# The up projection's norm row turned after its sixth weight piece

## The chip, the cores and the metric

The kernel runs on one core of a Trainium2 chip. A core has TensorE (PE, the matrix products), VectorE (DVE), ScalarE (ACT), GpSimd (POOL) and SyncE (SP, which here issues most transfers). The metric is the device time of one execution in microseconds, the median of several runs; the kernel before takes 1119.6 us.

## The reference

One layer of a hybrid encoder block on 256 tokens of 2048 features, in float32. The part around the change is the gated channel mixer, which starts with an RMS norm of the residual stream `h`:

```
def rmsnorm(x, g):
    y = xf * lax.rsqrt(jnp.mean(xf * xf, axis=-1, keepdims=True) + EPS)
    return (y * g.astype(F32)).astype(x.dtype)
def conv_glu(hn, w_up, conv_w, conv_b, w_down):
    up = hn @ w_up
    gate, val = jnp.split(up, 2, axis=-1)
    gate = dwconv_centred(gate, conv_w, conv_b)
    return (jax.nn.gelu(gate, approximate=True) * val) @ w_down
...
h = h + rmsnorm(mix @ w_out, mix_norm_post)
h = h + rmsnorm(conv_glu(rmsnorm(h, ffn_norm_pre), ...), ffn_norm_post)
```

`w_up` has 2 x 5632 columns. The gate half goes through a three-tap convolution over positions and a Gelu, and is multiplied by the value half. A mixer stands ahead of this part, the down projection and a gated per-layer embedding follow.

## The kernel before

**Precision.** Each float32 weight is split into a high part (rounded for the faster products, a cast on ScalarE, line 153) and a low part (the rest, a subtraction on VectorE, line 154). Two products, high by both parts of the activation (128x512) and low by the high part (128x256), stand for one float32 product.

**Pieces.** The up projection runs feature-major: features on partitions, the 256 tokens along the free axis. Its weights come in 176 pieces of 1024 columns of buffer. Four pieces (16 slices of 128 input features) make one block of 256 output features; `blocks` runs over slabs `s` of 512 features, first the two gate blocks `(s, 0, i)`, then the two value blocks `(s, 1, i)`. So pieces 0 to 3 are gate block 0 of slab 0 (tiles `ug_*`, results in `ga`), 4 to 7 gate block 1, and 8 to 15 the value blocks (`uv_*`, `va`). One transfer of 1 MB brings two pieces (`ug00r`, `ug01r`, `uv00r`, `uv01r`, two transfers each). There are three buffers for raw weights and five each for high and low parts (tags `raw`, `whi`, `wlo`), so a piece's high part takes over the buffer of the piece five before it. `next_part` splits a piece, five pieces ahead of its products; `feature_pairs` (line 355) issues the 16 products of a piece.

**The norm.** The products use `h` without the norm's factor per token; that factor is put on afterwards. `row_rstd` (line 398) squares and sums `h` per token on ScalarE (line 404) and takes the power -1/2 on POOL (line 381), with tokens on partitions. The gate needs the factor along the free axis. `along_tokens` (line 408) spreads each half over 128 columns (line 414, tile `rfbw`), turns it by a product with the identity (`mm`, line 90, tile `rfbp`), and copies it out (line 416, tile `rfb`). In the kernel before this is called ahead of the piece loop.

**A gate block's end.** `gate_out` adds the two partial results (lines 370 and 371) and multiplies by `rfb` (line 954). In the next block's first two passes of the loop come `gate_conv` (six ScalarE instructions, lines 961 to 963, and two VectorE additions, 964 and 965) and `gelu` (line 969). `value_out` multiplies the value by the gate. The value's factor is put on later, in the down projection.

**What sets the order.** Within `with in_order():` every instruction on ScalarE, VectorE and SyncE is tied to the one written before it on its engine. TensorE isn't in that list (`ORDERED`): its order is chosen by the scheduler when the kernel is built, under the data dependences and under `tc.issue_after(x)`, which ties what is issued inside it behind instruction `x`. `last["pe"]` is the product that was issued last. `jobs_at[n]` holds side work of pass `n`, block sums of later weights among it (`dnb`: fetch by SP, four additions at line 253, a store by POOL).

**Transfers ahead.** After the first split of the up projection SP's queue holds, in this order: `ug00r` twice, `ug01r` twice, two stores of `h` (`h_kept`), one of the embedding's half (`pl_kept`), `dnb`, `uv00r` twice, `dnb`, `uv01r` twice.

Of the kernel before, what the change touches and what calls it, by code (L numbers as in the profile page):

```python
# [11 lines left out]
F32 = mybir.dt.float32  # L12
F32R = mybir.dt.float32r
AF = mybir.ActivationFunctionType
ALU = mybir.AluOpType
ORDERED = (mybir.EngineType.Activation, mybir.EngineType.DVE, mybir.EngineType.SP)

P = 128
L = 256
# [34 lines left out]
def build(nc, a, out):  # L54
# [6 lines left out]
    with tile.TileContext(nc) as tc, \  # L61
# [9 lines left out]
        def ins(r):  # L71
            return getattr(r, "ins", r)
# [4 lines left out]
        def mid(name, dtype=F32):  # L77
            return gp.tile([P, 1024], dtype, tag="mid", bufs=3, name=name)
# [4 lines left out]
        def main(name):  # L83
            return [pm.tile([P, 512], F32, tag="main", name=f"{name}_{i}") for i in range(2)]

        def misc(name):
            return pc.tile([P, 512], F32, tag="misc", name=name)

        def mm(o, lhsT, rhs, start, stop):
            last["pe"] = ins(nc.tensor.matmul(o, lhsT, rhs, start=start, stop=stop, skip_group_check=True))  # L90
# [5 lines left out]
        ident = cp.tile([P, P], F32, name="ident")  # L96
# [9 lines left out]
        acc, acc2 = [main(f"dtu{t}") for t in range(2)], main("dtu2")  # L106
# [8 lines left out]
        last, sums_ = {}, {}  # L115
# [26 lines left out]
        def split(name, src, nel, cuts=()):  # L142

            if name in ready:
                return ready.pop(name)
            if name in spare:
                hi, lo = spare.pop(name)
            else:
                hi = wp.tile([P, 1056], F32R, tag="whi", bufs=5, name=f"{name}h")
                lo = wp.tile([P, 1056], F32R, tag="wlo", bufs=5, name=f"{name}l")  # L150
            for c0, c1 in zip((0, *cuts), (*cuts, nel)):
                s = slice(c0, c1)
                last["act"] = ins(nc.scalar.copy(hi[:, s], src[:, s]))  # L153
                last["dve"] = ins(nc.vector.tensor_sub(lo[:, s], src[:, s], hi[:, s].bitcast(F32)))
            return hi, lo

        def raw(name, src=None):
            r = wp.tile([P, 2048], F32, tag="raw", bufs=3, name=name)
            if src is not None:
                last["dma"] = load(r, src, True)  # L160
            return r
# [36 lines left out]
        @contextmanager  # L198
        def in_order():


            block = nc.cur_bb.bb.instructions
            seen = {i.name for i in block}
            yield
            for i in block:
                if i.name in seen or i.engine not in ORDERED:
                    continue
                if i.engine in chain:
                    tc.add_manual_dep(i, chain[i.engine].name,
                                      mybir.DependencyInfo(mybir.DependencyClass.NoSync, mybir.DependencyReason.DATA),  # L210
                                      reason="in_order")
                chain[i.engine] = i
# [142 lines left out]
        def feature_pairs(n, part, get, acc):  # L355

            wh, wl = part
            for kk in range(4):  # L360
                k = 4 * n + kk
                for f in range(2):
                    s = slice(kk * 256 + f * P, kk * 256 + (f + 1) * P)
                    mm(acc[f], wh[:, s], get.both(k), k == 0, False)
                    mm(acc[f][:, L:], wl[:, s], get(k)[0], False, k == NK - 1)

        def total(o, acc):

            for f in range(2):
                nc.scalar.copy(o[:, f * L:(f + 1) * L], acc[f][:, L:])  # L370
                nc.vector.tensor_add(o[:, f * L:(f + 1) * L], o[:, f * L:(f + 1) * L], acc[f][:, :L])
# [26 lines left out]
        def row_rstd(name, src):  # L398

            r = []  # L400
            for t in range(2):
                q = tiny(f"{name}q{t}", 1)
                junk = page(f"{name}j{t}")
                nc.scalar.activation(junk, src[t], AF.Square, accum_out=q)
                r.append(rms(f"{name}{t}", [q], 1.0 / D))
            return r

        def along_tokens(name, r):

            rb = sp.tile([P, L], F32, tag="rb", bufs=1, name=name)  # L410
            ps = misc(f"{name}p")
            for t in range(2):
                w = mid(f"{name}w{t}")
                nc.vector.tensor_copy(w[:, :P], r[t][:, 0:1].to_broadcast([P, P]))
                mm(ps[:, t * P:(t + 1) * P], w[:, :P], ident, True, True)
            nc.vector.tensor_copy(rb, ps[:, :L])
            return rb
# [283 lines left out]
        def job(f, *args):  # L701
            return lambda: f(*args)
# [75 lines left out]
        def gload(name, src):  # L778
            g = cp.tile([P, D], F32, tag="gain", name=name)
            load(g, src.partition_broadcast(P))  # L780
            return g
# [86 lines left out]
        for t in range(2):  # L868
            load(h[t], x[t * P:(t + 1) * P, :])
        hf = sublayer("wo", w_out, list(range(8, 16)) + list(range(8)), cat, gload("gmix", a["mix_norm_post"][0]), h,  # L870
                      V_FN, Pairs, ((5,), (2, 4)), Sums("cs", cat))
# [1 line left out]

        pl = [ple(0)]
        rf = row_rstd("rf", h)
        rfb = along_tokens("rfb", rf)
        h_kept = []
        for t in range(2):
            h_kept.append(dp.tile([P, D], F32, tag=f"h{t}", bufs=1, name=f"h_kept{t}"))
# [11 lines left out]
        for i, w_ in enumerate(which[2:] + which[:2]):  # L891
            fetch, add, store = block_sums(*w_, i >= len(which) - 2)
            n = 49 * i // 10 + 2
# [41 lines left out]
        blocks = [(s, v, i) for s in range(DFF // 512) for v in range(2) for i in range(2)]  # L935
        parts, slab = [], {}

        def next_part():

            n = len(parts)  # L940
            if n < NPIECES:
                s, v, i = blocks[n // 4]
                name = f"u{'gv'[v]}{s}{i}"
                if n % 2 == 0:
                    slab["raw"] = raw(f"{name}r{n // 2 % 2}", w_up[v, s, i, n // 2 % 2])
                parts.append(split(f"{name}{n // 2 % 2}_{n % 2}", slab["raw"][:, n % 2 * 1024:(n % 2 + 1) * 1024], 1024))

        def gate_out(s, i, acc):
            if i == 0:
                slab[s] = mid(f"gr{s}"), mid(f"fc{s}"), mid(f"ft{s}")  # L950
            o = slab[s][0][:, i * 512:(i + 1) * 512]
            total(o, acc)
            v = o.rearrange("p (f t) -> p f t", f=2)
            nc.vector.tensor_tensor(v, v, rfb.unsqueeze(1).to_broadcast([P, 2, L]), op=ALU.mult)

        def gate_conv(s, i):

# [13 lines left out]
        def value_out(s, i, acc):  # L971
# [4 lines left out]
            total(hd, acc)  # L976
            nc.vector.tensor_mul(hd, hd, slab[s][1][:, i * 512:(i + 1) * 512])

        with in_order():
            for _ in range(5):  # L980
                next_part()
            for n in range(NPIECES):
                s, v, i = blocks[n // 4]
                if n % 4 == 0:
                    acc = main(f"{'gv'[v]}a{s}{i}")
                feature_pairs(n % 4, parts[n], hf, acc)
                if n % 4 == 3:
                    (value_out if v else gate_out)(s, i, acc)
                next_part()
                if n >= 4 and n % 4 < 2 and blocks[n // 4 - 1][1] == 0:  # L990
                    (gelu if n % 4 else gate_conv)(blocks[n // 4 - 1][0], blocks[n // 4 - 1][2])
                for job in jobs_at[n]:
                    job()
# [98 lines left out]
        for half in range(2):  # L1092

            alt = [] if half else main(f"gts{half}")
            acc = [main(f"gt{half}{t}") for t in range(2)]
# [9 lines left out]
            for t in range(2):  # L1105
                for n, (o, c0) in enumerate(columns(acc[t])):
# [4 lines left out]
                    v = th[:, :c1 - c0]  # L1111
# [91 lines left out]
```

## Time and profile before

| what | us |
|---|---|
| median of 3 runs | 1119.6 (1119.28 to 1119.72) |
| the profiled execution | 1119.3 |
| its span in the trace | 1117.4 |
| TensorE busy | 1106.2 |
| VectorE busy | 946.9 |
| ScalarE busy | 718.0 |
| mean granted clock of TensorE | 0.998 |

The chain of waits, which goes back from the last instruction to what released each step, has 95% of its length on TensorE. Its pieces of gate and value blocks of the up projection take 43.4% of the span. One block of the steady part lies on it with 22.33 us per 128 products, which is two blocks of 64.

A row of the timeline gives the start in us, the duration in us, engine, line, operation, the tile written and the tiles read, and the shape and count; in brackets how long the engine had been idle and who released it. A TensorE duration includes the pipeline's fill, so that rows overlap: the pace is read from start to start. A row of a stage window gives the stretch, its length, the busy time (and instructions) of PE, its weight loads, DVE, ACT and POOL, the granted clock of TensorE, the DMA engines' share and GB/s. A row of the waits gives who waited for whom, total us, times and longest.

### The profile page before, as it was taken

To read this page: it belongs to the slowest core of one execution; us is meant where nothing else is said; L and a number is where in the kernel's file an instruction comes from. 1 tells how busy PE (TensorE), PEld (TensorE's weight loads), DVE (VectorE), ACT (ScalarE), POOL (GpSimd) and SP (SyncE) were. 2 spreads that over 40 slices of the span, in tenths; PEclk is the share of its full clock that TensorE was granted. 3 is DMA by queue.
4 is the path that set the end of the run, shared out by engine and by line. 5 is a ranking of instruction groups with operands and counts; after the bars stand their busy time and mean duration, and the time that the engine had idled before them with its cause. 6 is when DMAs were issued, how large, how long until landed. Compare 5 with 4: busy or idle time off the path is not lost.

```text
span 1117.4 us, 15979 instructions
## 1 busy us (share of the span) xinstructions
PE 1106.2 (99%) x5954; PEld 952.3 (85%) x5954; DVE 946.9 (85%) x1311; ACT 718.0 (64%) x1042; POOL 65.2 (6%) x134
## 2 busy tenths in 40 slices
PE   9999999999999999999999999999999999999997
PEld 9999988888888888888888888888888888877876
DVE  6468897799878898888878888889899999989795
ACT  7848663555775564665655646547689778867573
POOL 0200000100100000000000000000000000001001
PEclk9999999999999999999999999999999999999999
DMA  9752447454699999999899898999999799996663
GB/s 365 311 205 97 167 157 280 151 189 167 234 362 396 363 361 355 368 345 367 331 361 368 349 365 335 365 375 362 348 381 378 255 347 410 415 371 228 228 233 108
DMA packets 53503, 339.43 MB, mean 304 GB/s; under 512 B 5936, under 2 KB 6832, under 8 KB 19248
## 3 DMA queue, kind: packets, MB, share of 16 engines
q1 hardware_dynamic: 43488, 285.86, 66.2%
q0 software_dynamic: 9504, 51.91, 12.5%
q8 instruction: 47, 0.77, 0.3%
q10 hardware_dynamic: 432, 0.62, 0.2%
q14 instruction: 32, 0.26, 0.1%
HBM read 292.76 MB, written 45.61 MB: 303 GB/s over the span
## 4 chain that ended last, share of the span: by engine, by line
PE 95%; DVE 2%; ACT 2%; issue 1%; DMA 0%; POOL 0%; SPq 0%; POOLq 0%; ACTq 0%
PE va L90 22%; PE ga L90 21%; PE dna L90 12%; PE woa L90 7%; PE xbc L90 6%; PE gt L90 5%; PE z L90 4%; PE dtu L90 4%; PE dns L90 4%; PE dn0s L90 2%; PE dn1s L90 2%; PE ple L90 1%; PE pw L90 1%; PE yd L90 1%; DMA dtur<-w_dtu 0%
## 5 line engine op out<-in xcount | busy, mean ns | idle before, releaser
L90 PE MATMUL ga<-wox,ug_0h 128*128 128x512 f32 x352 | 125.5, 395 | 0.0
L90 PE MATMUL ga<-wox,ug_1h 128*128 128x512 f32 x352 | 125.1, 394 | 0.0
L90 PE MATMUL va<-wox,uv_0h 128*128 128x512 f32 x352 | 124.8, 393 | 0.0
L90 PE MATMUL va<-wox,uv_1h 128*128 128x512 f32 x352 | 124.7, 393 | 0.0
L90 PE MATMUL ga<-wox,ug_1l 128*128 128x256 f32 x352 | 99.2, 282 | 0.0
L90 PE MATMUL ga<-wox,ug_0l 128*128 128x256 f32 x352 | 99.1, 282 | 0.0
L90 PE MATMUL va<-wox,uv_0l 128*128 128x256 f32 x352 | 99.1, 281 | 0.0
L90 PE MATMUL va<-wox,uv_1l 128*128 128x256 f32 x352 | 98.9, 281 | 0.0
L253 DVE TENSOR_TENSOR dnb<-dnb 128x512 f32<-128x512 f32 x124 | 85.5, 690 | 3.2
L90 PEld LDWEIGHTS va<-wox,uv_0h 128*128 128x128 f32 x352 | 66.1, 188 | 15.0
L90 PEld LDWEIGHTS ga<-wox,ug_0h 128*128 128x128 f32 x352 | 66.1, 188 | 14.9
L90 PEld LDWEIGHTS ga<-wox,ug_1h 128*128 128x128 f32 x352 | 66.1, 188 | 14.9
L90 PEld LDWEIGHTS va<-wox,uv_1h 128*128 128x128 f32 x352 | 66.1, 188 | 14.9
L90 PEld LDWEIGHTS ga<-wox,ug_0l 128*128 128x128 f32 x352 | 66.2, 188 | 0.1
L90 PEld LDWEIGHTS va<-wox,uv_1l 128*128 128x128 f32 x352 | 66.2, 188 | 0.1
L90 PEld LDWEIGHTS ga<-wox,ug_1l 128*128 128x128 f32 x352 | 66.2, 188 | 0.0
L90 PEld LDWEIGHTS va<-wox,uv_0l 128*128 128x128 f32 x352 | 66.2, 188 | 0.0
L905 ACT CAST hs<-hid 128x512 fp32r<-128x512 f32 x44 | 27.3, 621 | 23.4 <-PE dna L90 23.1
L906 DVE TENSOR_TENSOR hs<-hid,hs 128x512 fp32r<-128x512 f32 x44 | 30.1, 685 | 8.3 <-ACT hs L905 8.3
L244 POOL DMA_DIRECT2D dns<-dnb x29 | 15.7, 540 | 318.4 <-DVE dnb L253 284.4
L90 PE MATMUL dna<-dn_0h,hs 128*128 128x512 f32 x104 | 33.1, 394 | 0.3 <-ACT dn_0h L153 0.3
L90 PE MATMUL dna<-dn_1h,hs 128*128 128x512 f32 x104 | 33.3, 393 | 0.0
(2164 smaller groups left out, 3168.4 us busy)
## 6 DMA issues: line engine op xcount, KB each, us to landing
dnb<-w_down SPq DMA_DIRECT2D x31, 1024.0 KB, 8.8
dns<-dnb POOLq DMA_DIRECT2D x29, 1024.0 KB, 5.3
hd<-hsum POOLq DMA_DIRECT2D x22, 512.0 KB, 8.2
zr<-w_z SPq DMA_DIRECT2D x8, 1024.0 KB, 5.0
dtur<-w_dtu SPq DMA_DIRECT2D x14, 528.0 KB, 8.4
wo0r<-w_out_ SPq DMA_DIRECT2D x7, 1024.0 KB, 4.9
dn1r<-w_down SPq DMA_DIRECT2D x7, 1024.0 KB, 6.8
wo1r<-w_out_ SPq DMA_DIRECT2D x6, 1024.0 KB, 4.9
```

Of the source, the lines that this page charges most:

```text
L90: last["pe"] = ins(nc.tensor.matmul(o, lhsT, rhs, start=start, stop=stop, skip_group_check=True))
L244: nc.gpsimd.dma_start(t, pg[0])
L253: nc.vector.tensor_add(v[:, i], v[:, i], v[:, j])
L905: nc.scalar.copy(t[:, :512], hid_part(k))
L906: nc.vector.tensor_sub(t[:, 512:], hid_part(k), t[:, :512].bitcast(F32))
```

## The change

The turned row is cut into three steps, `spread`, `turn` and `take`, which `norms_row` returns; nothing of it is issued ahead of the loop any more. `spread` (two copies on VectorE) is issued in pass 4, after that pass's split; `turn` (two products) in pass 5, behind the products of piece 5; `take` (the copy out) in pass 5 after its split. The products of piece 6 are tied behind the turning products. The norm of gate block 0 leaves `gate_out` and follows `take` in pass 5; its taps move from pass 4 to pass 6, its Gelu from pass 5 to pass 7. All other blocks keep their places; the norm is then read from `slab["rfb"]`. The spread row now takes the one buffer of tag `junk` in place of two tiles of `mid`.

```
-        rfb = along_tokens("rfb", rf)
+        def norms_row():
+            rb = sp.tile([P, L], F32, tag="rb", bufs=1, name="rfb")
+            ps = misc("rfbp")
+            w = sp.tile([P, 512], F32, tag="junk", bufs=1, name="rfbw")
+            def spread():
+                for t in range(2):
+                    nc.vector.tensor_copy(w[:, t * P:(t + 1) * P], rf[t][:, 0:1].to_broadcast([P, P]))
+            def turn():
+                with tc.issue_after(last["pe"]):
+                    for t in range(2):
+                        mm(ps[:, t * P:(t + 1) * P], w[:, t * P:(t + 1) * P], ident, True, True)
+            def take():
+                nc.vector.tensor_copy(rb, ps[:, :L])
+                slab["rfb"] = rb
+            return spread, turn, take
...
             total(o, acc)
-            v = o.rearrange("p (f t) -> p f t", f=2)
-            nc.vector.tensor_tensor(v, v, rfb.unsqueeze(1).to_broadcast([P, 2, L]), op=ALU.mult)
+            if s or i:
+                gate_norm(s, i)
+        def gate_norm(s, i):
+            v = slab[s][0][:, i * 512:(i + 1) * 512].rearrange("p (f t) -> p f t", f=2)
+            nc.vector.tensor_tensor(v, v, slab["rfb"].unsqueeze(1).to_broadcast([P, 2, L]), op=ALU.mult)
...
+        row = norms_row()
         with in_order():
...
-                feature_pairs(n % 4, parts[n], hf, acc)
+                with tc.issue_after(last["pe"]) if n == 6 else nullcontext():
+                    feature_pairs(n % 4, parts[n], hf, acc)
                 if n % 4 == 3:
                     (value_out if v else gate_out)(s, i, acc)
+                if n == 5:
+                    row[1]()
                 next_part()
-                if n >= 4 and n % 4 < 2 and blocks[n // 4 - 1][1] == 0:
+                if n == 4:
+                    row[0]()
+                elif n == 5:
+                    row[2]()
+                    gate_norm(0, 0)
+                elif n in (6, 7):
+                    (gelu if n == 7 else gate_conv)(0, 0)
+                elif n >= 8 and n % 4 < 2 and blocks[n // 4 - 1][1] == 0:
                     (gelu if n % 4 else gate_conv)(blocks[n // 4 - 1][0], blocks[n // 4 - 1][2])
```

## The prediction

> **What bounds the kernel now.** I read the engine totals first, then the chain of waits from 286 us on, then the waits of TensorE, then stage windows, and last each engine's timeline from 300 to 326 us.
>
> ```profile
> span 1117.4 us, 15979 instructions
> PE 1106.2 (99%) x5954; PEld 952.3 (85%) x5954; DVE 946.9 (85%) x1311; ACT 718.0 (64%) x1042; POOL 65.2 (6%) x134
> ```
> ```profile
> PE rfbp L90 <- DVE rfbw L414: 0.5, 1, 0.5
> ```
> ```profile
> 308.60:314.00 5.40, 5.40 (x33) 4.66 (x32) 3.14 (x6) 1.88 (x5) 0.74 (x2) 1.00 0.99 402
> 314.00:319.50 5.50, 5.50 (x33) 4.82 (x32) 2.60 (x3) 4.54 (x8) 0.00 (x0) 1.00 1.02 429
> 319.50:342.00 22.50, 22.50 (x131) 19.79 (x130) 21.78 (x28) 16.95 (x26) 1.33 (x2) 1.00 0.90 351
> 342.00:788.00 446.00, 446.00 (x2558) 391.49 (x2557) 377.81 (x514) 263.74 (x392) 23.39 (x44) 1.00 0.93 360
> ```
> TensorE (PE) is the bound. Its only wait near the change is 0.5 us for the spread row; from 308.6 to 788 us it never stops (first number after the length is PE's busy time). So no later hole can swallow a delay: what PE loses here moves the end. The DMA share, the last number but one, is 0.99 to 1.02 up to 319.5: the transfers are saturated.
>
> ```profile
> 307.13 0.40 PE L90 MATMUL ga<-wox,ug_0h 128*128 128x512 f32 x1
> 308.07 0.46 PE L90 MATMUL rfbp<-ident,rfbw 128*128 128x128 f32 x2 [0.54 <-DVE rfbw L414]
> 308.28 0.36 PE L90 MATMUL ga<-wox,ug_0l 128*128 128x256 f32 x1
> ...
> 310.23 0.49 PE L90 MATMUL rfbp<-ident,rfbw 128*128 128x128 f32 x2
> 310.47 0.48 PE L90 MATMUL ga<-wox,ug_0h 128*128 128x512 f32 x1
> ...
> 313.68 0.39 PE L90 MATMUL ga<-wox,ug_0h 128*128 128x512 f32 x1
> 313.91 0.28 PE L90 MATMUL ga<-wox,ug_0l 128*128 128x256 f32 x1
> 314.03 0.40 PE L90 MATMUL ga<-wox,ug_0h 128*128 128x512 f32 x1
> ```
> Durations overlap in the pipeline, so I price by start to start: a 512-wide product 0.23 us (313.68 to 313.91), a 256-wide one 0.12, a turning product 0.21 to 0.24. The row at 313.68 is the first of piece 6; a piece, eight of each kind, takes 2.8 us.
>
> **What is removed.** Between 307.36 (0.23 after the row at 307.13) and 313.68 PE spent 0.92 us up to 308.28 and 0.24 from 310.23 on the row. Both go from this place: piece 5 ends at 313.68 - 1.16 = 312.52. The 0.21 + 0.24 = 0.45 of products come back later; 0.71 is the most that the edit can win.
>
> **What is moved, and what it waits for.** PE is not in the hand-written order, so the compiled order of the changed kernel decides. Shortened, with the engine in front:
>
> ```
> PE   ... piece 5: ga_1<-wox,ug_1l
> PE   va_0<-wox,uv_0h [waits ACT]   va_1<-wox,uv_0h
> PE   va_0<-wox,uv_0l [waits DVE]   va_1<-wox,uv_0l   va_0 uv_0h   va_0 uv_0l   va_1 uv_0h
> PE   rfbp<-ident,rfbw [waits DVE]  rfbp<-ident,rfbw
> PE   piece 6, piece 7, the other 9 products of piece 8
> DVE  ug_1l, gr, gr, uv_0l (piece 8), uv_1l (piece 9), rfbw, rfbw, uv_0l (piece 10), rfb, gr norm
> ACT  gr, gr, uv_0h, uv_1h (8, 9), uv_0h (10), uv_1h (11), six taps
> ```
> Piece 6 is tied behind the turned row. Seven products of piece 8, not tied, were put ahead of the row; and on VectorE the two spreads stand behind the split of piece 9. So PE, which has pieces 6 and 7 ready to run, first waits for piece 8's weights and then for piece 9's split. When are those there?
>
> ```profile
> 305.24 0.43 SPq L120 DMA_DIRECT2D dnb<-w_down  x1
> 305.77 1.93 SPq L120 DMA_DIRECT2D uv00r<-w_up  x2
> ```
> ```profile
> DMA to landing us min/median/max: 9.0/9.8/10.6
> ```
> ```profile
> 314.89 1.05 ACT L153 CAST uv_0h<-uv00r 128x1024 fp32r<-128x1024 f32 x1 [4.41 <-DMA uv00r<-w_up]
> 316.80 0.60 ACT L961 ACTIVATE fc<-gr,vt 128x256 f32<-128x256 f32 x1
> ...
> 319.68 1.03 ACT L153 CAST uv_0h<-uv00r 128x1024 fp32r<-128x1024 f32 x1
> ```
> ```profile
> 307.69 0.23 DVE L414 COPY rfbw<-rf0r 128x128 f32<-128x128 f32 x1 [1.65 <-POOL rf0r L381]
> ...
> 315.98 1.22 DVE L154 TENSOR_TENSOR uv_0l<-uv00r,uv_0h 128x1024 fp32r<-128x1024 f32 x1 [2.28 <-ACT uv_0h L153]
> 317.12 1.22 DVE L154 TENSOR_TENSOR uv_1l<-uv00r,uv_1h 128x1024 fp32r<-128x1024 f32 x1
> ...
> 321.88 2.86 DVE L253 TENSOR_TENSOR dnb<-dnb 128x512 f32<-128x512 f32 x4
> ```
> The transfer uv00r is issued at 305.77 behind pl_kept and dnb and lands 9.0 us later; ScalarE stood idle 4.41 us for it. The edit changes no place and no wait in SP's queue, and the work of ScalarE and VectorE that frees its buffer and makes the value stored ahead of it lies before the first edited instruction. I keep the landing.
>
> Step by step: uv_0h is there at 314.89 + 1.05 = 315.94, PE starts at 316.0 (312.52 to 316.0: 3.5 us idle). Two 0.23 products, to 316.46. uv_0l is done at 315.98 + 1.22 = 317.20, so PE goes on at 317.25 (0.8 idle) with 0.12 + 0.12 + 0.23 + 0.12 + 0.23 = 0.82, to 318.07. The split of piece 9 starts at 317.12; the next instruction follows 1.14 later, as 317.12 follows 315.98: the first spread runs 318.26 to 318.49. Before, the turning product came 0.15 after the spread's end (307.69 + 0.23 = 307.92, to 308.07): now 318.64 (0.6 idle). Two of them, 0.45: piece 6 starts at 319.09 instead of 313.68, 5.41 later, but with 4 x 0.23 + 3 x 0.12 = 1.28 of piece 8 done. **Net 5.41 - 1.28 = +4.13 us.** The same by idle time: 3.5 + 0.8 + 0.6 = 4.9, less the 0.71 won, is 4.2. Bounds: the two uv00r transfers took 9.0 and 10.6 us, so a first one as slow as the second would add 1.6 us, and one 0.8 faster would take 0.8 off (every step behind the landing moves with it). The one issue that the edit brings forward, uv01r (its buffer no longer waits for a split behind the turned row), stands behind uv00r in the queue, so I take the 9.0.
>
> **What is late next, and what is free.** The six taps (316.80 to 319.68, 2.9 us), the norm and the Gelu move back by two pieces on ScalarE and VectorE. They hide behind the splits' lead of five pieces. The tightest is piece 11, whose high part needs the buffer of piece 6: free at 319.09 + 2.8 = 321.9, cast to 322.9 (1.05). Its low part stands behind the row's copy, the norm and the block sums (2.86), which have all run by then, and is done near 325. PE wants it after piece 7, the rest of 8, 9 and 10: 319.09 + 5.6 + 1.5 + 5.6 = 331.8, 7 us later. Piece 12's cast waits for the taps and two copies, until about 328, and is wanted at 334.6. So I price them at nothing; without the lead, the 2.9 us of taps would be paid. The stores on POOL's queue follow block sums that come about 1 us later or sooner, with nobody waiting for them in this stage.
>
> **The clock.** PE would work only 1.7 us of the 6.6 from 312.52 to 319.09. What does this trace do with so little work?
>
> ```profile
> 1.39 3.40 PE L109 MATMUL dtu<-ident 128*128 128x128 f32 x16 [1.39 <-POOL ident masks.py:199]
> 4.65 0.59 PE L90 MATMUL dtu<-dtu0h,hnh 128*128 128x352 f32 x2
> ...
> 293.60 0.60 PE L391 MATMUL woxt<-ident,h 128*128 128x128 f32 x4
> 293.95 0.48 PE L90 MATMUL ga<-wox,ug_0h 128*128 128x512 f32 x1
> ```
> ```profile
> 1021.55:1024.96 3.41, 2.62 (x16) 1.97 (x15) 3.41 (x6) 2.17 (x4) 0.00 (x0) 1.00 0.41 173
> 1106.88:1110.30 3.42, 2.66 (x18) 1.83 (x16) 1.51 (x4) 1.48 (x5) 0.82 (x2) 1.00 0.04 14
> 1110.30:1113.71 3.41, 1.13 (x2) 0.30 (x2) 2.08 (x3) 1.00 (x3) 0.55 (x1) 1.00 0.34 121
> 1113.71:1117.40 3.69, 0.00 (x0) 0.00 (x0) 0.00 (x0) 0.00 (x0) 0.00 (x0) 0.50 0.55 174
> ```
> The first transposes took 3.26 / 16 = 204 ns each, those at 293.60 0.35 / 4 = 88: a cold start at under half speed for some 3.3 us. At the end the granted clock fell to 0.50 after 3.41 us with 1.13 of work (a third), though PE had rested only 1.2 us; with 2.62 of 3.41 it held. In the new hole any stretch of 3.4 us that begins between 311.4 and 314.5 holds at most 1.1 us of work: if the clock is decided stretch by stretch, 3.1 of 3.4 ways in which they can lie drop it. So I expect a half-clock spell of some 3.3 us. It costs half of the work in it: at most 1.7, nothing where it falls on PE's waits. It begins between 314.8 and 317.9, and up to 319.1 most of it is waits: I take 0.9, about half, bounds 0 and 2.0 (1.7, and 0.3 for the products ahead of the row, which then hold it up).
>
> The Trainium skill, "TensorE: Matmul & The Clock Gate", Part 1, says that the clock drops to half after at least one idle window of about 3.4 us on a free-running grid. Read as a window with no work at all, it would hardly ever fit in the 3.5 us wait, and the sum would stay +4.1 (rival 1); the tail here dropped after a window a third busy, so I side with the row.
>
> **Sum.** +4.13 + 0.9 = +5.0. On the profiled execution's 1119.3 us (span 1117.4): 1124.3; the median of the runs shown lies 0.3 higher, so 1124.6.
>
> **Rivals.**
> 1. The stall comes, the clock holds: +4.1, 1123.7. For it: the third of work that dropped the clock is one case, at the end of the program. Against it: the stall has even less. Chance 0.25.
> 2. Faster: uv00r lands early enough. Without waits PE reaches the turned row at 312.52 + 1.28 = 313.80 instead of 318.64, so the landing must come 4.8 us sooner, 4.2 us after its issue; then the 0.7 is won: 1118.9. From 4.9 us after issue on (4.1 sooner) it is no loss. For it: ug01r landed nearly as fast on an emptier queue,
>
> ```profile
> DMA to landing us min/median/max: 4.7/5.2/5.7
> ```
> (the view of ug01r, issued at 288 and before). Against it: the stored value and dnb, 1 MB each, stand ahead in the same queue, at a DMA share of 0.99. Chance 0.03; with 0.02 for a landing in between that just cancels.
> 3. The half clock lasts a second spell, since PE's slower work in the first counts too little: another 1.7, 1119.6 + 4.1 + 0.9 + 1.7 = 1126.3. For it: at the start it needed 3.3 us of steady work. Against it: from 319.1 on the work is steady. Chance 0.10.
>
> **How the numbers follow.** The forecast (stall and one spell) has 0.60, rival 1 0.25, rival 3 0.10, rival 2 with its middle 0.05. The range: low, rival 1 less the 0.8 of a faster landing, 1122.9; high, rival 3, 1126.3. About 0.2% (2.2 us) is what a measurement of this kernel can tell from no change: slower than 1121.8 holds all but 0.05, so faster 0.03, same 0.02, slower 0.95.
>
> **What would show it.** In the changed kernel's trace: PE's waits should list va for uv_0h (some 3.5 us), va for uv_0l (0.8) and rfbp for rfbw (0.6), where the old 0.5 is gone; piece 6 should start near 319 or later, with no further PE wait up to the down projection, and all later rows shifted alike. The granted clock between 314 and 323 should show a stretch at 0.50. It is wrong if uv00r lands elsewhere than about 314.9, if piece 6 precedes the row, or if a split of pieces 9 to 13 stops PE.

## The result

The changed kernel takes 1124.4 us (median of 6, 1123.8 to 1125.2), the kernel before 1119.5 (median of 6, 1119.0 to 1119.7). The ratio is 1.0045, with a 95% interval of 1.0035 to 1.0055: slower by 4.9 us.

The profile of the changed kernel has rows that answer to those shown of the kernel before. First come the head of its page and its list of TensorE's waits in the whole program (who waited for whom: total us, times, longest).

```profile
span 1122.0 us, 15982 instructions
...
PE 1107.7 (99%) x5954; PEld 953.8 (85%) x5954; DVE 947.0 (84%) x1311; ACT 718.3 (64%) x1042; POOL 65.2 (6%) x134
```
```profile
PE va L90 <- ACT uv_0h L153: 3.4, 1, 3.4
PE gof L90 <- ACT godg L1114: 1.9, 1, 1.9
...
PE va L90 <- DVE uv_0l L154: 0.3, 1, 0.3
```

The old wait for the spread row is gone. In its place stands the longest wait of the program, for piece 8's high part, and a short one for its low part. The number of instructions on PE is the same, its busy time is 1.5 us longer: the same work ran slower somewhere. PE's timeline shows where.

```profile
311.87 0.39 PE L90 MATMUL ga<-wox,ug_1h 128*128 128x512 f32 x1
312.10 0.28 PE L90 MATMUL ga<-wox,ug_1l 128*128 128x256 f32 x1
315.78 0.93 PE L90 MATMUL va<-wox,uv_0h 128*128 128x512 f32 x2 [3.40 <-ACT uv_0h L153]
317.04 0.79 PE L90 MATMUL va<-wox,uv_0l 128*128 128x256 f32 x2 [0.33 <-DVE uv_0l L154]
317.63 0.63 PE L90 MATMUL va<-wox,uv_0h 128*128 128x512 f32 x1
318.06 0.41 PE L90 MATMUL va<-wox,uv_0l 128*128 128x256 f32 x1
318.27 0.63 PE L90 MATMUL va<-wox,uv_0h 128*128 128x512 f32 x1
318.70 1.03 PE L90 MATMUL rfbp<-ident,rfbw 128*128 128x128 f32 x4
319.41 0.56 PE L90 MATMUL ga<-wox,ug_0h 128*128 128x512 f32 x1
```

Piece 5 ends, 3.4 us of nothing, seven products of piece 8, the turned row, and only then piece 6. From 317.63 to 318.06 a 512-wide product takes 0.43 us from start to start, where 0.23 is the pace before and after. The stage windows have the reason, in the granted clock (the last number but two) and PE's busy time (the first after the length):

```profile
312.75:316.17 3.42, 0.39 (x2) 0.30 (x2) 0.41 (x1) 1.49 (x2) 0.00 (x0) 1.00 1.00 422
316.17:319.58 3.41, 3.08 (x12) 2.40 (x11) 3.36 (x5) 1.57 (x2) 0.00 (x0) 0.50 1.01 425
319.58:342.00 22.42, 22.42 (x130) 19.68 (x130) 18.64 (x26) 17.11 (x27) 1.33 (x2) 1.00 0.77 300
342.00:788.00 446.00, 446.00 (x2558) 391.47 (x2557) 376.84 (x513) 263.83 (x393) 23.41 (x44) 1.00 0.92 358
```

For 3.41 us the clock was granted at half; then PE runs without a hole through the up projection, as before. The other two engines and the queue:

```profile
314.68 1.04 ACT L153 CAST uv_0h<-uv00r 128x1024 fp32r<-128x1024 f32 x1 [4.41 <-DMA uv00r<-w_up]
...
322.50 1.05 ACT L153 CAST uv_1h<-uv00r 128x1024 fp32r<-128x1024 f32 x1 [4.25 <-PE ga L90]
```
```profile
316.90 1.22 DVE L154 TENSOR_TENSOR uv_1l<-uv00r,uv_1h 128x1024 fp32r<-128x1024 f32 x1
318.04 0.22 DVE L884 COPY rfbw<-rf0r 128x128 f32<-128x128 f32 x1
```
```profile
305.57 1.93 SPq L120 DMA_DIRECT2D uv00r<-w_up  x2
```

The spread runs right behind the split of piece 9, which follows the landing of uv00r, and the landing is where it was: ScalarE's cast of uv_0h, which waits for it, starts at 314.68 in place of 314.89, 0.21 us earlier, and the row of squares that stands ahead of the edit is 0.21 earlier too (306.73 and 306.94).

**Where in the span the time went.** Two rows, the second squaring of `h` and the first product of the down projection, bracket the stage, and leave out the few tenths by which executions differ before it.

```profile
306.73 1.98 ACT L404 ACTIVATE rfj<-h 128x2048 f32<-128x2048 f32 x1
```
```profile
792.91 0.62 PE L90 MATMUL dna<-dn_0h,hs 128*128 128x512 f32 x2
```

Here the bracket is 486.18 us; in the kernel before it runs from 306.94 to 788.30, 481.36. So 4.82 us, all of the loss, lie in it. What follows to the end of the span takes 329.1 us in both.

### The profile page after: what moved, and what is told of

The parts are those of the page before. It is cut to its first block, busy times and chain, and to the rows that moved or that the text cites. A ratio compares the mean times of both kernels' runs of the same rounds, so it can differ in the third digit from the quotient of the medians.

```text
span 1122.0 us, 15982 instructions
## 1 busy us (share of the span) xinstructions
PE 1107.7 (99%) x5954; PEld 953.8 (85%) x5954; DVE 947.0 (84%) x1311; ACT 718.3 (64%) x1042; POOL 65.2 (6%) x134
## 4 chain that ended last, share of the span: by engine, by line
PE 94%; DVE 2%; ACT 2%; DMA 2%; issue 0%; POOL 0%; POOLq 0%; ACTq 0%
PE va L90 22%; PE ga L90 21%; PE dna L90 12%; PE woa L90 7%; PE xbc L90 6%; PE gt L90 5%; PE z L90 4%; PE dns L90 4%; PE dtu L90 4%; PE dn0s L90 2%; PE dn1s L90 2%; PE ple L90 1%; DMA uv00r<-w_up 1%; DMA dtur<-w_dtu 1%; PE pw L90 1%; PE yd L90 1%
```

## The experiments

The table has the median of each kernel beside that of the kernel before on the same chip, the ratio with its 95% interval, and the bracket of its profile against the 481.36 of before (worked out from the same two rows).

| run | median us | before | ratio, interval | bracket |
|---|---|---|---|---|
| changed kernel again | 1124.41 | 1119.55 | 1.0046, 1.0033 to 1.0058 | +4.77 |
| filled wait, 14 | 1123.48 | 1119.55 | 1.0034, 1.0022 to 1.0047 | +3.67 |
| early spread | 1118.67 | 1119.55 | 0.9993, 0.9984 to 1.0001 | -0.78 |
| untied | 1118.59 | 1119.55 | 0.9992, 0.9983 to 1.0001 | -0.78 |
| piece 8 held back | 1127.01 | 1119.57 | 1.0068, 1.0051 to 1.0085 | +7.53 |
| late taps alone | 1119.44 | 1119.57 | 1.0000, 0.9991 to 1.0009 | +0.06 |
| late store | 1119.57 | 1119.57 | 0.9999, 0.9990 to 1.0008 | -0.01 |
| filled, order kept, 1 | 1124.64 | 1119.56 | 1.0045, 1.0032 to 1.0059 | +4.61 |
| filled, order kept, 13 | 1123.82 | 1119.56 | 1.0039, 1.0026 to 1.0051 | +4.09 |
| early spread again | 1118.83 | 1119.56 | 0.9993, 0.9985 to 1.0002 | -0.78 |

**The changed kernel again.**

> The changed kernel once more, beside the next three. Theory: 4.9 us over the kernel before (1124.4 beside 1119.5). The half-clock spell begins somewhere between 314.8 and 318 in every execution but not at the same place, so its span should vary by some tenths of a us more than the kernel before does.

It came as expected, with the half-clock spell from 316.12 to 319.54. Its times vary more, too: the standard deviation of its five is 0.64 us, that of the 21 of the kernel before 0.27. The granted clock of each execution points to a reason. The two slowest, 1125.24 and 1125.46, have a mean of 0.994, the other three, 1124.11 to 1124.41, have 0.997. A mean of 0.994 (0.9945 at most) is at least 12.3 us at half in a span of 1123.5. The profiles of all kernels show 3.1 to 5.7 us at half at the end of the program, so more than one window of 3.41 us is left for elsewhere. A second window at half in the stall, as in the prediction's third rival, would explain the 1.1 us by which these two are slower; no trace of them shows where it lay.

**Which step makes the stall: the place of the spread.**

```
                 if n == 5:
                     row[1]()
+                if n == 3:
+                    row[0]()
                 next_part()
-                if n == 4:
-                    row[0]()
-                elif n == 5:
+                if n == 5:
```

> The changed kernel with one step moved: the two spreads in pass 3 ahead of that pass's split, not in pass 4 behind it. Everything else (turn, take, norm, taps, Gelu) stays late. The compiled order then has the turned row right behind piece 5 and piece 8 whole behind piece 7. Theory, the place of the spreads on VectorE makes the stall: no wait on PE, the old 0.54 gone too, 0.7 us under the kernel before: 1118.8 (bounds 1118.3 and 1119.5). Rival, the late taps, norm and Gelu or the new buffers cost the time: stays near 1124.

Its PE timeline around piece 5:

```profile
312.97 0.28 PE L90 MATMUL ga<-wox,ug_1l 128*128 128x256 f32 x1
313.09 0.61 PE L90 MATMUL rfbp<-ident,rfbw 128*128 128x128 f32 x4
313.45 0.47 PE L90 MATMUL ga<-wox,ug_0h 128*128 128x512 f32 x1
```

The last product of piece 5, 0.12 us later the turned row, 0.36 us after it piece 6; PE has no wait in the stage, not even the old one, and the clock stays full. The turn, the norm, the taps and the Gelu stand in the same passes as in the changed kernel, so none of them cost the time: two copies of 0.22 us, too late on VectorE, did. The spread's place also decides the compiled order on PE: with the early one the seven products of piece 8 are not put ahead. Repeated, to narrow the interval:

> The kernel with the early spread once more, to narrow its interval: 0.7 to 0.9 us under the kernel before, 1118.7.

Both times the bracket is 0.8 us shorter than before and the median 0.7 to 0.9 lower, but the intervals of both ratios just reach 1. That it beats the kernel before is shown in the profile's stage, and not beyond the interval in the total.

**Or the tie.**

```
-                with tc.issue_after(last["pe"]) if n == 6 else nullcontext():
+                with nullcontext():
```

> The changed kernel without the tie that holds piece 6 behind the turned row; the spreads stay behind piece 9's split. The compiled order has pieces 6 and 7 first, then ten products of piece 8, then the row. Theory, the tie and the late spread make the stall together: PE reaches piece 8 near 318, after its weights (316), and the row near 320, after the spread (318.5): no wait, 1118.8 (bounds 1118.3 and 1119.5). Rival, the late spread alone costs: PE waits for rfbw and the time stays above 1121.

As expected: the spread is as late as in the changed kernel, at 318.30, but PE has pieces 6, 7 and ten products of 8 ahead of the turned row, which comes at 319.84. So late spread and tie cost only together: the tie turns a late row, which no one yet needs, into a wait of all of PE.

**Or the seven products of piece 8.**

```
-                with tc.issue_after(last["pe"]) if n == 6 else nullcontext():
+                with tc.issue_after(last["pe"]) if n in (6, 8) else nullcontext():
```

> The changed kernel with a second tie, piece 8 behind piece 7, so that no product of piece 8 stands ahead of the turned row. PE then goes from piece 5 (312.3) straight into the wait for the spread (318.6, behind the splits of pieces 8 and 9). Theory, the place of the spread on VectorE behind the landing of uv00r sets when piece 6 starts, and the seven products ahead of it are not the cause but 1.28 us done in the wait: piece 6 starts near 319 as before the tie, 5.4 us late, plus a longer half-clock spell (1 to 2.5 us, nothing keeps PE busy): 1119.5 + 5.4 + 1.5 = 1126.4, bounds 1125.5 and 1128. Rival, the seven products ahead of the row are the cause: faster than the changed kernel, below 1123.

Slower yet, by 7.5 us. Its timeline and windows:

```profile
319.16 1.19 PE L90 MATMUL rfbp<-ident,rfbw 128*128 128x128 f32 x4 [6.00 <-DVE rfbw L884]
320.00 0.77 PE L90 MATMUL ga<-wox,ug_0h 128*128 128x512 f32 x1
```
```profile
313.44:316.85 3.41, 0.00 (x0) 0.00 (x0) 0.34 (x1) 1.41 (x2) 0.00 (x0) 1.00 1.01 428
316.85:320.27 3.42, 1.11 (x5) 1.14 (x6) 3.42 (x5) 1.62 (x2) 0.00 (x0) 0.50 1.01 426
320.27:323.68 3.41, 3.41 (x12) 2.92 (x11) 3.17 (x7) 0.00 (x0) 0.00 (x0) 0.50 1.01 423
323.68:327.00 3.32, 3.32 (x21) 2.89 (x21) 1.87 (x2) 2.29 (x4) 0.78 (x1) 1.00 0.60 252
```

Without the seven products the waits merge into one of 6.0 us for the spread. So the products put ahead do not make the stall; they are work that is done in it (1.28 us by the prediction's sum). The bracket is 2.71 us longer than the changed kernel's, and how much of that is the missing work and how much the clock, this run can't tell. For the half clock lasts two windows: the first held only 1.11 us of work and didn't lift it. That is the mechanism of the prediction's third rival, in a kernel that leaves PE emptier than the changed one.

**What sets the time of the row: the landing.**

```
-        load(pl_kept, pl[0])
...
+        jobs_at[9].append(lambda: load(pl_kept, pl[0]))
```

> The changed kernel with one store moved: the embedding's half is stored in pass 9, not ahead of the loop, so SP's queue no longer waits for its last copy (304.7) before it issues dnb and uv00r. Theory, the landing of uv00r sets every step of the stall: the transfer can be issued from about 300 on, when its buffer is free, and lands near 308; then uv_0h is there by 311.3, the spread by 313.8, PE waits 0.3 us at most, and the time is 1119.0 (bounds 1118.5 and 1120). Rival, the order on PE and VectorE costs whatever the landing: stays near 1124.

The queue of this kernel, and its one wait of PE in the stage:

```profile
300.88 4.17 SPq L120 DMA_DIRECT2D uv00r<-w_up  x2
305.10 0.42 SPq L120 DMA_DIRECT2D dnb<-w_down  x1
```
```profile
PE rfbp L90 <- DVE rfbw L884: 0.3, 1, 0.3
```
```profile
313.08 0.62 PE L90 MATMUL va<-wox,uv_0h 128*128 128x512 f32 x2
313.70 0.51 PE L90 MATMUL va<-wox,uv_0l 128*128 128x256 f32 x2
...
314.40 0.40 PE L90 MATMUL va<-wox,uv_0h 128*128 128x512 f32 x1
315.07 0.68 PE L90 MATMUL rfbp<-ident,rfbw 128*128 128x128 f32 x4 [0.27 <-DVE rfbw L884]
```

With the order on PE and VectorE untouched and one store of 1 MB out of the way, uv00r goes out at 300.88 in place of 305.57, and the stall is all but gone. The time is 0.6 us over what was expected, inside the bounds. PE's rows account for most of that. The seven products take from 313.08 to 314.63, 1.55 us and not 1.28, since the low part of piece 8 holds them up. The row starts 0.44 after that, at 315.07. Together 0.71, where 0.3 was expected.

**The rest of the change.**

```
-                if n >= 4 and n % 4 < 2 and blocks[n // 4 - 1][1] == 0:
+                if n in (6, 7):
+                    (gelu if n == 7 else gate_conv)(0, 0)
+                elif n >= 8 and n % 4 < 2 and blocks[n // 4 - 1][1] == 0:
```

> The kernel before with one part of the change alone: taps of gate block 0 in pass 6 and its Gelu in pass 7; the row and the norm stay ahead of the loop. Theory, this part is hidden by the splits' lead of five pieces: within 0.5 us of the kernel before, 1119.5, no new wait on PE. Rival, the later taps and table load hold up splits: a new PE wait at pieces 9 to 13 and over 1121.

On top of the kernel before, the late taps and Gelu cost nothing (interval 0.9991 to 1.0009), and PE has no new wait in the stage.

**The price of the clock.** Filling products in the wait keep PE at work without being needed by anything. They use columns of the row's buffer that the row leaves free.

```
                 if n == 5:
+                    for _ in range(FILL):
+                        with tc.issue_after(last["pe"]):
+                            mm(row_ps[0][:, 256:384], ident, ident, True, True)
                     row[1]()
```

> 14 products of the identity with itself, into unused columns of the turned row's buffer, are put between piece 5 and the seven products of piece 8 (14 x 0.22 = 3.1 us in a wait of 3.4). Theory, the wait for piece 8's weights and the clock are two terms: the first is unchanged, the granted clock stays at 1.00, piece 6 starts some 0.5 us sooner than in the changed kernel's profile, time about 4.2 us over the kernel before, 0.5 to 0.9 under the changed kernel. Rival, the clock costs nothing: same time as the changed kernel. Rival, any work added to PE is paid: 3.1 us slower, 1127.5.

The clock stayed at 1.00 and the time fell by 0.9 us, the upper end of what was expected. But the filling also changed the compiled order, with ten products of piece 8 ahead of the row and not seven, so that 0.47 us more work was done in the waits. The two cannot be told apart in this run. In the next pair the order is fixed by a tie inside piece 8 (its products from the eighth on stand behind piece 7), and only the number of filling products differs.

> The run with 14 filling products had ten products of piece 8 ahead of the turned row, the changed kernel seven: two things differed. Here the order is that of the changed kernel (seven, by a tie inside piece 8) with one filling product, 0.23 us in a wait of 3.4. Theory: like the changed kernel, 1124.4, half-clock spell and all. It is the partner of the next run. Rival, the order of piece 8 alone made the gain of the filled run: the same time as the next run.

> The same with 13 filling products (13 x 0.235 = 3.05 us), nothing else changed. Theory, the spell costs some 0.7 us (in the changed kernel's profile piece 6 starts 12.68 us after the second row of squares begins, and 12.1 would follow from the waits alone): no granted clock under 1.00, 0.7 us (0.4 to 1.0) faster than the partner with one product: 1123.7. Rival, the clock costs nothing: no difference.

The waits of the kernel with 13, the rows behind them, and its windows over the stretches:

```profile
PE va L90 <- DVE uv_0l L154: 0.5, 1, 0.5
PE va L90 <- ACT uv_0h L153: 0.5, 1, 0.5
PE rfbp L90 <- DVE rfbw L888: 0.2, 1, 0.2
```
```profile
316.26 0.73 PE L90 MATMUL va<-wox,uv_0h 128*128 128x512 f32 x2 [0.46 <-ACT uv_0h L153]
317.52 0.51 PE L90 MATMUL va<-wox,uv_0l 128*128 128x256 f32 x2 [0.53 <-DVE uv_0l L154]
...
318.21 0.39 PE L90 MATMUL va<-wox,uv_0h 128*128 128x512 f32 x1
318.79 0.71 PE L90 MATMUL rfbp<-ident,rfbw 128*128 128x128 f32 x4 [0.18 <-DVE rfbw L888]
```
```profile
315.00:316.20 1.20, 0.80 (x8) 0.61 (x6) 0.00 (x0) 1.04 (x2) 0.00 (x0) 1.00 0.98 416
316.20:319.60 3.40, 2.63 (x13) 1.80 (x14) 3.36 (x5) 2.00 (x3) 0.00 (x0) 1.00 1.02 431
```

With one product the clock is at half from 316.10 to 319.52; with 13 it holds, and the bracket is 0.52 us shorter. The changed kernel and its repeat, which have the same order and no filling product, are 0.73 and 0.68 above the kernel with 13. So in the profiled executions the spell costs 0.5 to 0.7 us. In all three kernels with a spell it began at nearly the same time (316.17, 316.12, 316.10); what it costs when it begins elsewhere, these profiles don't show. The medians of the pair differ by 0.82, but they are of five runs each and the intervals of the two ratios overlap. The stall by itself, with a full clock, costs +4.09 in the bracket.

## Why the prediction was right

It gave 1124.6 in a range of 1122.9 to 1126.3; measured are 1124.4. By its own steps:

1. **The bound.** PE has no hole up to 788 us that could swallow a delay: shown by the 446.00 of 446.00 us in the window up to 788 and by the 329.1 us that follow in both kernels.
2. **What is won.** The old wait was priced at no more than 0.71. The kernels in which nothing replaces it have a bracket 0.78 us shorter, a little above that ceiling; in the medians it is 0.7 to 1.0.
3. **The order and what it waits for.** The seven products, the wait for uv_0h (3.5 expected, 3.40 found), for uv_0l (0.8 and 0.33) and for the spread (0.6 and none listed). With the clock held by 13 filling products the last two are listed as 0.53 and 0.18. Part of that is the way of counting: the list counts from the modelled end of a product, the prediction from start to start, and so the wait for uv_0l is 0.80 (316.26 + 2 x 0.23 = 316.72, to 317.52) as expected, and the one for the spread 0.35 (318.21 + 0.23 = 318.44, to 318.79), shorter than expected. The rest of the difference in the changed kernel is the half clock, which stretched the products ahead of them into the waits.
4. **The stall.** +4.13 against +4.09 in the kernel with 13 filling products. That the two agree to 0.04 is partly chance, since single terms were off by more (the wait for the spread by 0.25). That the spread's place makes it, the early spread shows; that the tie is its other half, the untied kernel; that the landing of uv00r times it, the late store. The landing stayed where it was in the kernel before.
5. **The clock.** The half-clock spell came, with the 3.41 us that the tail had led to expect. Its price was set at 0.9 and is 0.5 to 0.7 in the profiles, so more of it fell inside PE's waits than the half that was assumed. The Trainium skill, "TensorE: Matmul & The Clock Gate", Part 1, has the clock drop to half after at least one idle window. Taken as a window with no work at all, that rule would have kept the clock: the window ahead of the drop held 0.39 us of products here, 0.12 in the repeat and 1.13 at the tail of the kernel before. The measurement decides.
6. **What was priced at nothing.** Late taps and Gelu: 0.06 us in the bracket, measured alone. Piece 11's cast started at 322.50, where 321.9 was worked out, and held up no product.

The first rival (clock holds) falls with the windows. The second (early landing) is true as a mechanism and false as a case, as the late store shows. The third (two spells) came in the profile of the kernel with piece 8 held back. Both profiles of the changed kernel show one spell, but by the granted clocks two executions of its repeat probably had a second one, at some 1.1 us and not the 1.7 that the rival was priced at.

## What to carry to other kernels

Before a tie is put on an engine that is never idle, follow what the tied-to instruction needs back through each in-order queue: here two copies of 0.22 us stood behind two splits, and those behind a 1 MB transfer that lands 9 us after its issue. Read the compiled order as well as the source, since an engine left to the scheduler fills the room by its own guess, and that order changed with the place of a copy on another engine. A stall of PE costs its length and, where it leaves a window of 3.41 us less than about half full (1.53 us of products and less dropped the clock here, 1.97 and more kept it), a spell at half clock on top.

## What the hardware showed that was not expected

The granted clock changes on a regular grid. In every profile the times between changes are whole multiples of one window: in the changed kernel 3.41 us at half, 310.61 at full ahead of it (91 times 3.4133) and 798.72 behind it (234 times), and in the kernel with piece 8 held back 6.83 at half. The windows on this grid bound the amount of work that decides. In and near the stall, 0.00, 0.12, 0.30 and 0.39 us of products in a window dropped the clock, and 2.43 (with 13 filling products) kept it. The ends of the programs narrow it, because the grid lay differently over them in each execution. Two windows in a row of the kernel with late taps alone, then two of the repeated early spread:

```profile
1107.84:1111.26 3.42, 1.97 (x12) 1.14 (x10) 0.88 (x4) 1.10 (x6) 1.37 (x3) 1.00 0.01 2
1111.26:1114.67 3.41, 1.12 (x2) 0.30 (x2) 2.06 (x3) 0.97 (x2) 0.00 (x0) 1.00 0.55 184
```
```profile
1108.53:1111.94 3.41, 1.52 (x4) 0.30 (x2) 2.21 (x5) 1.24 (x4) 0.55 (x1) 1.00 0.01 2
1111.94:1115.35 3.41, 0.31 (x1) 0.00 (x0) 0.71 (x2) 0.59 (x1) 0.00 (x0) 0.50 0.93 305
```

After 1.97 us of products the next window still has the full clock, after 1.52 it has half. The kernel with piece 8 held back kept it with 2.06, and three more kernels lost it with 1.52 or 1.53. So a window need not be empty to drop the clock; less than about half of it in work was enough, and what decides between 1.53 and 1.97 us no run here shows. With the clock already at half, 1.11 us (piece 8 held back) and 1.37 (the end of the untied kernel) did not lift it, and 3.08 (stretched by the half clock) did.
